# Keys and values of a differential-attention layer: turned by VectorE and DMA in place of TensorE, with the weighted sums as fences in the order of two engines

## The chip, the cores and the metric

The kernel runs on one core of one Trainium2 chip. The metric is the device time of one execution in microseconds (us), the median of several runs; less is better.

## What is computed

One inference step of a trunk of two layers, for a prompt of 512 tokens and 32 sampled tokens, in float32. Layer 0 mixes tokens with RWKV-7, layer 1 with differential attention; both have cross-attention to a memory, a gate and an output projection. The change concerns layer 1 and the norm ahead of it:

```python
def diff_layer(x, mk, mv, k_past, v_past, layer_idx, norm_w, w_out, w_in, lq1, lk1, lq2, lk2, subln):
    h = rmsnorm(x, norm_w)
    q, k, v, qm, gate = jnp.split(h @ w_in, [MIX_W, 2 * MIX_W, 3 * MIX_W, 3 * MIX_W + MEM_W], axis=-1)
    ...
        blocks.append(diff_attention(q[:, s:e], k_all[:, :past + e], v_all[:, :past + e], q_pos, k_pos, lam))
    o = jnp.concatenate(blocks, axis=1)
    o = rmsnorm(o, subln) * (1.0 - lam_init)
    y_mem = mem_attention(qm, mk, mv)
    out = jnp.concatenate([o.reshape(B, T, MIX_W).astype(x.dtype), y_mem], axis=-1) * jax.nn.silu(gate)
    return x + out @ w_out, k, v
```

There are 12 heads of width 128 (two maps of 64 each); `diff_attention` is `softmax(q1 k1) - lam * softmax(q2 k2)`, applied to `v`. Keys and values are outputs too, with the token first and then the head: 512 x 12 x 128 for the prompt and 32 x 12 x 128 for the samples.

## The kernel before

All 544 tokens (512 of the prompt, `TP`, and 32 samples, `TS`) stand as columns; features stand on the 128 partitions. A projection is made in blocks of 128 output features. For float32 accuracy both operands are split into a high and a low part (`hh` and `hl` for the input, `whi` and `wlo` for the weights), and a block is 2 halves of 272 tokens x 8 slices x 3 matmuls = 48 matmuls into `ps_g` (`steps`, line 348). `block` (line 1887) issues these 48 and puts other work between them: `pieces` is a list of (place, step), and a step is issued before the matmul of that place. At the end of a block `used` (line 283) has the weights of a coming block split, ScalarE rounding `whi` and VectorE subtracting to `wlo`, and has SP issue the loads of a later one into `raw`, of which there are five buffers.

`groups` (line 1898) runs layer 1 in three groups of four heads. For a head it issues a block of keys, one of queries and one of values. The head's own attention is a generator (`steps` in `diff_head`, line 2056), which is advanced by the pieces: four steps in its block of values, five in the next head's block of keys and four in the next head's block of queries (gate and memory blocks take their place after the fourth head). The steps of a head, before:

- the keys are rounded, and their parts sent to the other half of the partitions (`kh`, a DMA) and subtracted (`kz`, VectorE);
- in the values' block: `turned(k, 4)`, the scores of the first and second 128 tokens (`scores`: four matmuls, the maximum on VectorE, the exponential on ScalarE, and `combine` on VectorE), then the samples' scores and `probs(0)`, TensorE transposes of the combined probabilities into `aT`;
- in the next block, at places 10, 20, 30, 40 and 45: `turned(v, 5)` and the samples' keys and values; `scores(2)` and `probs(1)`; `weighted(0)`; `scores(3)`; `probs(2)`;
- in the block after that, at 6, 18, 30 and 42: `weighted(1)`, `weighted(2)`, `probs(3)`, `weighted(3)`.

`turned` (line 2017) makes four TensorE transposes of 128 x 128 into `ps_kv`, a ScalarE copy to `kt` or `vt`, and one DMA from there to the output. `ps_kvs` takes two more transposes a head, of the last 128 columns of keys and values, from which ScalarE copies the 32 samples to `vs`. `weighted(t)` (line 2047) sums t + 1 products of `aT` and `vt` in the one buffer of `ps_o`; VectorE copies it to `ot`, and ScalarE sums its squares.

Which order do the instructions take? In layer 0 every instruction is tied to the one before on its engine (`tie`, line 123, while `ordered` is true). In layer 1 `ordered` is false: the framework's scheduler places each engine's instructions, from the order of their issue and what it thinks of their times. Line 106 in the profile stands for all four queues' instructions, since one helper issues them; they are told apart by tile.

Between the layers the input of layer 1 is normalised, slice by slice of 128 features: `h` on VectorE, `hh` rounded by ScalarE, `hl` subtracted by POOL (line 1763). The projections of the memory, with weights of their own to split, are issued between the slices.

Of the kernel before, what the change touches and what calls it, by code (L numbers as in the profile page):

```python
# [97 lines left out]
class Queue:  # L98


    def __init__(self, trunk, engine):
        self.trunk, self.engine, self.last = trunk, engine, None

    def __getattr__(self, name):
        issue = getattr(self.engine, name)
# [3 lines left out]
class Trunk:  # L109
# [13 lines left out]
    def tie(self, queue, ins):  # L123

        if self.ordered:
            if queue.last is not None:
                self.order(ins, queue.last)
            queue.last = ins
        return ins

    def rsqrt(self, y, x, pool, tag):
# [1308 lines left out]
    def layer0(self, mem):  # L1440
# [245 lines left out]
        with ExitStack() as ctx:  # L1686
# [70 lines left out]
            for k in range(KT):  # L1757
                h = p.tile([P, T], F32, tag="hn", name="hn", bufs=HNB)
                for q, c, n in ((0, 0, TP), (1, TP, TS)):
                    self.ve.scalar_tensor_tensor(h[:, c : c + n], self.x1[:, k, c : c + n], self.nw[1][:, k : k + 1],  # L1760
                                                   pr[q][:, :n], ALU.mult, ALU.mult)
                self.ae.copy(self.hh[:, k, :], h[:])
                nc.gpsimd.tensor_tensor(self.hl[:, k, :], h[:], self.hh[:, k, :].bitcast(F32), ALU.subtract)  # L1763
                next(kv, None)
            for _ in kv:
                pass
# [17 lines left out]
    def layer1(self):  # L1784
# [7 lines left out]
        with ExitStack() as ctx:  # L1792
            with ExitStack() as c2:
                self.dfp = p = self.pool("df", 1, ctx=c2)
                m1 = c2.enter_context(ExitStack())
                mp = self.pool("mem1a", 1, ctx=m1, side="right")

                nlam = self.nlam
                self.qs = [p.tile([P, P], F32, name=f"qs{i}") for i in range(2)]
                for t in self.qs:  # L1800
                    nc.gpsimd.memset(t[:], 0.0)
                self.kz = [p.tile([P, 2, T], F32R, name=f"kz{i}") for i in range(2)]
                for t in self.kz:
# [12 lines left out]

                self.groups(w, p, mp, nlam, aside, free)
# [80 lines left out]
    def groups(self, w, p, mp, nlam, aside, free):  # L1898

        late = []  # L1900
        for hg in range(3):
# [5 lines left out]
            def gate(c0, pieces):  # L1907
                self.gates += 1
                sg, _, evac = self.gate_evac(self.gates)
                self.block(w, 3 * MIXW + 512 + c0, evac, pieces)  # L1910
                return sg

            for j, (parts, it) in enumerate(heads):
                h = 4 * hg + j
                before = step(prev, 10, 20, 30, 40, 45) if j else late
                k, q, v = parts()
                self.block(w, MIXW + h * P, k, before)
                if not j and hg == 2:
                    free()
                next(it)  # L1920
                self.block(w, h * P, q, step(prev, 6, 18, 30, 42) if j else ())
                if j:
                    aside()
                if j == 3 and hg < 2:
                    mem = [self.mem_turn(1, 2 * hg + i, mp) for i in range(2)]
                    for _ in range(2):
                        next(mem[0][1])
                self.block(w, 2 * MIXW + h * P, v, step(it, 6, 16, 28, 40))
                prev = it
            end = self.diff_end(gr, nlam)  # L1930
            fin = lambda j, at: (at, lambda: end.send((j, sgs[j])))
            g0 = 4 * hg * P
            sgs.append(gate(g0, step(prev, 10, 20, 30, 40, 45)))
            if hg == 2:
                sgs.append(gate(g0 + P, step(prev, 6, 18, 30, 42)))
                aside()
                sgs.append(gate(g0 + 2 * P, step(end, 2, 10, 18) + [fin(0, 22), fin(1, 36)]))
                sgs.append(gate(g0 + 3 * P, [fin(2, 16)]))
                fin(3, 0)[1]()
                break  # L1940
# [8 lines left out]
                    st["evac"](ps, v)  # L1949
                return evac  # L1950

            self.block(w, 3 * MIXW + st0["c"], query(st0), step(m0, 2) + step(prev, 6, 18, 30, 42))
# [16 lines left out]
    def diff_group(self, hg, p):  # L1969

        a, gr = self.a, {"hg": hg, "on": []}
        gr["ck"] = p.tile([P, 4, P], F32, tag="ck", name="ck")
        gr["cv"] = p.tile([P, 4, P], F32, tag="cv", name="cv")
        gr["ckT"] = p.tile([P, 4, P + TS], F32, tag="ckT", name="ckT")
        gr["vs"] = p.tile([TS, 2, 4, P], F32, tag="vs", name="vs")
        gr["ssb"] = p.tile([P, 2, 160], F32, tag="ssb", name="ssb")
        gr["ss"] = p.tile([P, 3, 16], F32, tag="oss", name="oss")
        return gr
# [6 lines left out]
    def diff_head(self, gr, j, p, nlam):  # L1985
# [29 lines left out]
            return keys, queries, values  # L2015

        def turned(x, n):
            t = p.tile([P, 4, P], F32, tag="kt" if n == 4 else "vt", name="kt" if n == 4 else "vt", bufs=n - 3)
            ps = self.psm.tile([P, 512], F32, tag="m", name="ps_kv")
            for i in range(4):  # L2020
                self.te.transpose(ps[:, i * P : i * P + P], x[:, i * P : i * P + P], self.ident[:])
            self.ae.copy(t[:], ps[:].rearrange("p (j c) -> p j c", j=4))
            self.se.dma_start(o[n][0, 0, :, h, :].rearrange("(i p) d -> p i d", p=P), t[:])
            return t

        def scores(t):
            n, S = (t + 1) * P, []
# [11 lines left out]
        def probs(t):  # L2039
            n = (t + 1) * P  # L2040
            ps = self.psm.tile([P, 512], F32, tag="m", name="ps_aT")
            for i in range(t + 1):
                self.te.transpose(ps[:, i * P : i * P + P], st["pt", t][:, 0, i * P : i * P + P], self.ident[:])
            st["aT", t] = p.tile([P, 512], F32, tag="aT", name="aT", bufs=2)
            self.ae.copy(st["aT", t][:, :n], ps[:, :n])

        def weighted(t):
            aT, ot = st["aT", t], st["ot"]
            po = self.psx.tile([P, 512], F32, tag="x", name="ps_o")
            for i in range(t + 1):  # L2050
                self.te.matmul(po[:, :P], aT[:, i * P : i * P + P], st["vt"][:, i, :], start=i == 0, stop=i == t)
            self.ve.tensor_copy(ot[:, t, :], po[:, :P])
            jk = p.tile([P, P], F32, tag="jk", name="jk", bufs=2)
            self.ae.activation(jk[:], ot[:, t, :], AF.Square, accum_out=gr["ss"][:, 0, 4 * j + t : 4 * j + t + 1])

        def steps():
# [26 lines left out]
            yield  # L2083
            if j == 0:
                self.cached(gr, "v")
            st["vt"] = turned(st["v"], 5)
            ps = self.psm.tile([P, 512], F32, tag="m", name="ps_kvs")
            for i, x in enumerate((k, st["v"])):
                self.te.transpose(ps[:, i * P : i * P + P], x[:, T - P :], self.ident[:])
            self.ae.copy(gr["vs"][:, :, j, :], ps[P - TS :, :256].rearrange("p (j c) -> p j c", j=2))  # L2090
            st["ot"] = p.tile([P, 4, P], F32, tag="ot", name="ot", bufs=4)
            gr["on"].append(st["ot"])
            yield
            scores(2)
            probs(1)
            yield
            weighted(0)
            yield
            scores(3)
            yield  # L2100
            probs(2)
            yield
            weighted(1)
            yield
            weighted(2)
            yield
            probs(3)
            yield
            weighted(3)
# [4 lines left out]
    def diff_end(self, gr, nlam):  # L2114
# [1 line left out]
        hg, p, ssb, vs, ss, o = gr["hg"], self.dfp, gr["ssb"], gr["vs"], gr["ss"], self.o  # L2116
        _, srs = self.softmax([ssb[:, m, :] for m in range(2)], P + TS, p, ssb)
        self.combine(ssb, srs, P + TS, nlam)
        for i, n in ((0, 10), (1, 11)):
            self.se.dma_start(o[n][0, 0, :, 4 * hg : 4 * hg + 4, :], vs[:, i])  # L2120
        self.ve.tensor_scalar(ss[:, 1, :], ss[:, 0, :], 1.0 / P, EPS, ALU.mult, ALU.add)
        self.rsqrt(ss[:, 2, :], ss[:, 1, :], p, "nt16")
        ps = self.psm.tile([P, 512], F32, tag="m", name="ps_saT")
        self.te.transpose(ps[:, :P], ssb[:, 0, :P], self.ident[:])
        self.te.transpose(ps[:TS, P : 2 * P], ssb[:, 0, P:160], self.ident[:])
        aT = p.tile([P, 512], F32, tag="aT", name="aTs", bufs=2)
        self.ae.copy(aT[:, :P], ps[:, :P])
        self.ae.copy(aT[:TS, P : 2 * P], ps[:TS, P : 2 * P])
        yield
# [4 lines left out]
                             tile_position=(0, 32 * j))  # L2134
        for j in range(4):
            rj = slice(32 * j, 32 * j + 32)
            self.te.matmul(po[rj, :P], aT[:TS, P + 32 * j : P + 32 * j + 32], vs[:, 1, j, :], start=False, stop=True,
                             tile_position=(0, 32 * j))
        os_ = p.tile([P, P], F32, tag="os", name="os")
        self.ve.tensor_copy(os_[:], po[:, :P])  # L2140
# [105 lines left out]
```

## Time and profile before

| | us |
|---|---|
| median of 3 runs | 1371.52 (1371.49 to 1371.97) |
| the profiled execution | 1371.42 |
| its span, first to last instruction | 1369.2 |
| POOL `hl<-hn,hh`, 8 times | 12.2 in all, 1.536 each |
| ScalarE `kt<-ps_kv`, 12 times | 0.580 each |
| ScalarE `vt<-ps_kv`, 12 times | 0.588 each |
| the granted clock of TensorE | 0.998 of full speed |

The profile names engines: PE is TensorE's matmuls, PEld its weight loads, DVE VectorE, ACT ScalarE, POOL GpSimd, SP the queue that issues the DMAs. A row of the timeline gives the start, the duration, the engine, the line, the operation with the tiles that it writes and reads, the shape and a count; idle time of the engine before it, and what ended that, stand in brackets. A matmul's duration is longer than the distance to the next one, as matmuls are pipelined: its price is read from starts.

### The profile page before, as it was taken

The page shows a single profiled execution, that of the slowest core. Times are in us where ns is not written, and L with a number is a line of the kernel's source. Part 1 is how long each engine was busy: PE and PEld are TensorE (multiplying, and loading weights), DVE is VectorE, ACT ScalarE, POOL GpSimd, SP SyncE. Part 2 cuts the span into 40 slices and gives each one's busy share as a digit, 9 for nine tenths or more (in the row PEclk, how much of TensorE's full clock was granted, in tenths as well). Part 3 has the DMA queues.
Part 4 walks back from the last instruction along what each step waited for, and adds up shares of the span by engine and source line. Part 5 has one row for each costly group of instructions (what it writes and reads, how often), then busy time and mean ns, then how long its engine had stood idle before and what let it go on. Part 6 is the DMA issues. An engine that isn't in the chain of part 4 may idle for free. (4 is left out here: it accounts for less than half of the span.)

```text
span 1369.2 us, 31861 instructions
## 1 busy us (share of the span) xinstructions
PE 1339.3 (98%) x11845; PEld 1283.9 (94%) x11845; DVE 939.7 (69%) x2353; ACT 822.6 (60%) x2288; POOL 381.9 (28%) x841
## 2 busy tenths in 40 slices
PE   8999999999999999999999999999999999999997
PEld 6988899999999998988999989999999999999997
DVE  5776788888888888667744667775567747667443
ACT  5766777877778777656433466654566537665222
POOL 2138667766686667600000120000000001002000
PEclk9999999999999999999999999999999999999999
DMA  7452322333323332432555563332333323332322
GB/s 224 146 140 70 77 71 57 94 86 74 88 67 84 88 88 64 142 87 76 173 142 147 148 184 88 100 102 82 101 95 94 90 82 94 97 97 79 93 78 73
DMA packets 276964, 139.06 MB, mean 102 GB/s; under 512 B 75769, under 2 KB 265730, under 8 KB 276810
## 3 DMA queue, kind: packets, MB, share of 16 engines
q1 hardware_dynamic: 276746, 137.01, 36.0%
q8 instruction: 94, 1.54, 0.5%
q14 instruction: 60, 0.49, 0.1%
q10 hardware_dynamic: 64, 0.02, 0.0%
HBM read 110.72 MB, written 22.91 MB: 98 GB/s over the span
## 5 line engine op out<-in xcount | busy, mean ns | idle before, releaser
L106 PE MATMUL ps_g<-hh,whi 128*128 128x272 f32 x1808 | 539.7, 299 | 1.0 <-DVE ats L106 0.7
L106 PE MATMUL ps_g<-hh,wlo 128*128 128x272 f32 x1808 | 534.8, 297 | 1.6 <-DVE wlo L106 1.5
L106 PE MATMUL ps_g<-hl,whi 128*128 128x272 f32 x1808 | 532.4, 295 | 0.6 <-DVE hl L106 0.3
L106 PEld LDWEIGHTS ps_g<-hh,whi 128*128 128x128 f32 x1808 | 341.2, 189 | 5.1 <-DVE ats L106 0.9
L106 PEld LDWEIGHTS ps_g<-hh,wlo 128*128 128x128 f32 x1808 | 340.6, 189 | 4.7 <-DVE wlo L106 2.5
L106 PEld LDWEIGHTS ps_g<-hl,whi 128*128 128x128 f32 x1808 | 341.1, 189 | 2.8 <-DVE hl L106 1.3
L106 DVE TENSOR_TENSOR wlo<-raw,whi 128x512 fp32r<-128x512 f32 x314 | 220.1, 712 | 118.3 <-ACT whi L106 114.7
L106 ACT CAST whi<-raw 128x512 fp32r<-128x512 f32 x314 | 188.9, 619 | 115.8 <-PE ps_g L106 62.4
L868 POOL TENSOR_TENSOR tm<-u,m 102x84 f32<-102x84 f32 (+23 forms) x341 | 147.8, 433 | 115.4 <-DMA m<-sc 69.5
L870 POOL TENSOR_TENSOR u<-u,tm 102x84 f32<-102x84 f32 (+23 forms) x341 | 151.6, 445 | 26.6
L106 PE MATMUL ps_g<-hi,wlo 128*128 128x272 f32 x512 | 147.8, 289 | 1.2 <-DVE wlo L106 1.2
L106 PE MATMUL ps_g<-hi,whi 128*128 128x272 f32 x512 | 147.7, 289 | 0.0
L106 PE MATMUL ps_g<-lo,whi 128*128 128x272 f32 x512 | 147.4, 288 | 0.0
L1339 POOL TENSOR_TENSOR lo<-og,hi 128x544 fp32r<-128x544 f32 x8 | 13.2, 1649 | 357.7 <-ACT hi L106 357.2
L106 PEld LDWEIGHTS ps_g<-hi,wlo 128*128 128x128 f32 x512 | 96.4, 188 | 1.7 <-DVE wlo L106 1.6
L106 PEld LDWEIGHTS ps_g<-hi,whi 128*128 128x128 f32 x512 | 96.5, 189 | 0.0
L106 PEld LDWEIGHTS ps_g<-lo,whi 128*128 128x128 f32 x512 | 96.4, 188 | 0.0
L106 ACT ACTIVATE pt<-ps_s,snm 128x128 f32<-128x128 f32 (+3 forms) x96 | 51.0, 532 | 41.7 <-DVE snm L106 41.6
L1763 POOL TENSOR_TENSOR hl<-hn,hh 128x544 fp32r<-128x544 f32 x8 | 12.2, 1536 | 211.4 <-ACT hh L106 211.3
L106 DVE SCALAR_TENSOR_TENSOR SB<-ps_c,dl,sd 64x64 f32<-64x64 f32 x168 | 47.4, 282 | 26.4 <-PE ps_c L106 21.2
L106 ACT COPY sv<-ps_c 64x64 f32<-64x64 f32 x192 | 39.6, 206 | 32.7 <-PE ps_c L106 30.8
L106 ACT ACTIVATE sg<-ps_g 128x272 f32<-128x272 f32 x64 | 25.2, 394 | 41.0 <-PE ps_g L106 38.3
(400 smaller groups left out, 2564.4 us busy)
## 6 DMA issues: line engine op xcount, KB each, us to landing
raw<-in_rw_in_dram SPq DMA_DIRECT2D x114, 256.0 KB
raw<-in_df_in_dram SPq DMA_DIRECT2D x112, 256.0 KB
raw<-in_w_out_dram SPq DMA_DIRECT2D x64, 256.0 KB
oscr<-sg SPq DMA_DIRECT2D x16, 272.0 KB
lo<-oscr SPq DMA_DIRECT2D x16, 272.0 KB
m<-sc SPq DMA_DIRECT2D x33, 128.0 KB
raw<-in_w_mem_v_dram SPq DMA_DIRECT2D x16, 256.0 KB
kh<-kh SPq DMA_DIRECT2D x24, 136.0 KB
```

Source lines behind the costliest of these rows:

```text
L106: return lambda *a, **k: self.trunk.tie(self, issue(*a, **k))
L868: nc.gpsimd.tensor_tensor(tm[:, :n, :wd], u3[:, :n, kx : kx + 1].to_broadcast(sh), m3[:, kx : kx + 1, kx + 1 :].to_broadcast(sh), ALU.mult)
L870: nc.gpsimd.tensor_tensor(u3[:, :n, kx + 1 :], u3[:, :n, kx + 1 :], tm[:, :n, :wd], ALU.add)
L1339: (self.nc.gpsimd if g % 2 and self.o1 else self.ve).tensor_tensor(lo[:], t, hi[:].bitcast(F32), ALU.subtract)
L1763: nc.gpsimd.tensor_tensor(self.hl[:, k, :], h[:], self.hh[:, k, :].bitcast(F32), ALU.subtract)
```

## The change

- **Keys and values.** `turned` makes no TensorE transposes any more. VectorE transposes the 512 prompt columns in blocks of 32 x 32, each in its place, and the 32 sample columns into `new`. Four DMAs, one for each 32 features, write 128-byte pieces and put the blocks in their places: for the keys straight to the output, for the values to a scratch in DRAM (`vscr`, one of two by head). `fetched` reads the values back from there to `vt`, and the values' output is written from `vt`. The samples' values go by four DMAs (`samples`) to `vs`, once a group; their keys go to the output by four DMAs at the end of a group.
- **Order.** The last matmul of each `weighted` is kept as `pin` of TensorE's queue, and its copy as `pin` of VectorE's: every later instruction of that queue is ordered behind it.
- **Places.** In the next block the steps stand at 4, 9, 30 and 44: `turned(v, 5)`; `scores(2)` and `probs(1)`; `fetched` (in the group's last head `samples` as well) and `scores(3)`; `probs(2)`. In the block after at 14, 24, 34 and 46: `weighted(0)` and the values' output; `weighted(1)`; `weighted(2)` and `probs(3)`; `weighted(3)`.
- **Buffers.** Three `aT` for two. The cached keys `ck` and the turned values share one buffer, `vb`.
- **Norm.** `hl` is subtracted by VectorE.

```diff
@@ class Queue, Trunk.tie
-        self.trunk, self.engine, self.last = trunk, engine, None
+        self.trunk, self.engine, self.last, self.pin = trunk, engine, None, None
...
             queue.last = ins
+        elif queue.pin is not None:
+            self.order(ins, queue.pin)
         return ins
@@ layer0, norm
-                nc.gpsimd.tensor_tensor(self.hl[:, k, :], h[:], self.hh[:, k, :].bitcast(F32), ALU.subtract)
+                self.ve.tensor_tensor(self.hl[:, k, :], h[:], self.hh[:, k, :].bitcast(F32), ALU.subtract)
@@ layer1
+                self.vscr = [self.dp.tile([TP, P], F32, name=f"vscr{i}") for i in range(2)]
@@ groups (the gate and memory blocks that take the same steps likewise)
-                before = step(prev, 10, 20, 30, 40, 45) if j else late
+                before = step(prev, 4, 9, 30, 44) if j else late
...
-                self.block(w, h * P, q, step(prev, 6, 18, 30, 42) if j else ())
+                self.block(w, h * P, q, step(prev, 14, 24, 34, 46) if j else ())
@@ diff_group
-        gr["ck"] = p.tile([P, 4, P], F32, tag="ck", name="ck")
+        gr["ck"] = p.tile([P, 4, P], F32, tag="vb", name="ck")
...
-        gr["vs"] = p.tile([TS, 2, 4, P], F32, tag="vs", name="vs")
+        gr["vs"] = p.tile([TS, 4, P], F32, tag="vs", name="vs")
+        gr["new"] = p.tile([P, 2, 4, TS], F32, tag="new", name="new")
@@ diff_head
         def turned(x, n):
-            t = p.tile([P, 4, P], F32, tag="kt" if n == 4 else "vt", name="kt" if n == 4 else "vt", bufs=n - 3)
-            ps = self.psm.tile([P, 512], F32, tag="m", name="ps_kv")
-            for i in range(4):
-                self.te.transpose(ps[:, i * P : i * P + P], x[:, i * P : i * P + P], self.ident[:])
-            self.ae.copy(t[:], ps[:].rearrange("p (j c) -> p j c", j=4))
-            self.se.dma_start(o[n][0, 0, :, h, :].rearrange("(i p) d -> p i d", p=P), t[:])
+            t = p.tile([P, 4, P], F32, tag="kt" if n == 4 else "vb", name="kt" if n == 4 else "vb")
+            t = t[:].rearrange("p j c -> p (j c)")
+            self.ve.transpose(t, x[:, :TP])
+            self.ve.transpose(gr["new"][:, n - 4, j, :], x[:, TP:])
+            to = o[4][0, 0, :, h, :] if n == 4 else self.vscr[h % 2][:]
+            to = to.rearrange("(b i) (a c) -> a i b c", i=TS, c=TS)
+            for a in range(4):
+                r = slice(TS * a, TS * a + TS)
+                self.se.dma_start(to[a], t[r, :].rearrange("i (b c) -> i b c", c=TS))
+
+        def fetched():
+            t = p.tile([P, 4, P], F32, tag="vt", name="vt", bufs=2)
+            self.se.dma_start(t[:], self.vscr[h % 2][:].rearrange("(i p) d -> p i d", p=P))
             return t
+
+        def samples():
+            for a in range(4):
+                r = slice(TS * a, TS * a + TS)
+                self.se.dma_start(gr["vs"][:, :, r], gr["new"][r, 1])
...
         def weighted(t):
...
-                self.te.matmul(po[:, :P], aT[:, i * P : i * P + P], st["vt"][:, i, :], start=i == 0, stop=i == t)
-            self.ve.tensor_copy(ot[:, t, :], po[:, :P])
+                mm = self.te.matmul(po[:, :P], aT[:, i * P : i * P + P], st["vt"][:, i, :], start=i == 0, stop=i == t)
+            cp = self.ve.tensor_copy(ot[:, t, :], po[:, :P])
+            self.te.pin, self.ve.pin = mm, cp
...
-            st["vt"] = turned(st["v"], 5)
-            ps = self.psm.tile([P, 512], F32, tag="m", name="ps_kvs")
-            for i, x in enumerate((k, st["v"])):
-                self.te.transpose(ps[:, i * P : i * P + P], x[:, T - P :], self.ident[:])
-            self.ae.copy(gr["vs"][:, :, j, :], ps[P - TS :, :256].rearrange("p (j c) -> p j c", j=2))
+            turned(st["v"], 5)
...
             scores(2)
             probs(1)
             yield
-            weighted(0)
-            yield
+            st["vt"] = fetched()
+            if j == 3:
+                samples()
             scores(3)
             yield
             probs(2)
             yield
+            weighted(0)
+            self.se.dma_start(o[5][0, 0, :, h, :].rearrange("(i p) d -> p i d", p=P), st["vt"][:])
+            yield
             weighted(1)
             yield
             weighted(2)
-            yield
             probs(3)
@@ diff_end
-        for i, n in ((0, 10), (1, 11)):
-            self.se.dma_start(o[n][0, 0, :, 4 * hg : 4 * hg + 4, :], vs[:, i])
+        self.se.dma_start(o[11][0, 0, :, 4 * hg : 4 * hg + 4, :], vs[:])
+        for a in range(4):
+            r = slice(TS * a, TS * a + TS)
+            self.se.dma_start(o[10][0, 0, :, 4 * hg : 4 * hg + 4, r], gr["new"][r, 0])
```

More of the change, by code (lines that the diff above doesn't have):

```diff
@@ L1932, in groups @@
             g0 = 4 * hg * P
-            sgs.append(gate(g0, step(prev, 10, 20, 30, 40, 45)))
+            sgs.append(gate(g0, step(prev, 4, 9, 30, 44)))
             if hg == 2:
-                sgs.append(gate(g0 + P, step(prev, 6, 18, 30, 42)))
+                sgs.append(gate(g0 + P, step(prev, 14, 24, 34, 46)))
                 aside()
@@ L1950, in query @@
                 return evac
-            self.block(w, 3 * MIXW + st0["c"], query(st0), step(m0, 2) + step(prev, 6, 18, 30, 42))
+            self.block(w, 3 * MIXW + st0["c"], query(st0), step(m0, 2) + step(prev, 14, 24, 34, 46))
             sgs.append(gate(g0 + P, step(end, 8, 20, 44)))
@@ L2043, in probs @@
                 self.te.transpose(ps[:, i * P : i * P + P], st["pt", t][:, 0, i * P : i * P + P], self.ident[:])
-            st["aT", t] = p.tile([P, 512], F32, tag="aT", name="aT", bufs=2)
+            st["aT", t] = p.tile([P, 512], F32, tag="aT", name="aT", bufs=3)
             self.ae.copy(st["aT", t][:, :n], ps[:, :n])
@@ L2125, in diff_end @@
         self.te.transpose(ps[:TS, P : 2 * P], ssb[:, 0, P:160], self.ident[:])
-        aT = p.tile([P, 512], F32, tag="aT", name="aTs", bufs=2)
+        aT = p.tile([P, 512], F32, tag="aT", name="aTs", bufs=3)
         self.ae.copy(aT[:, :P], ps[:, :P])
@@ L2136, in diff_end @@
             rj = slice(32 * j, 32 * j + 32)
-            self.te.matmul(po[rj, :P], aT[:TS, P + 32 * j : P + 32 * j + 32], vs[:, 1, j, :], start=False, stop=True,
+            self.te.matmul(po[rj, :P], aT[:TS, P + 32 * j : P + 32 * j + 32], vs[:, j, :], start=False, stop=True,
                              tile_position=(0, 32 * j))
```

## The prediction

> **What bounds the kernel now.** I read the page first, then the busy times by stage, then TensorE's waits, then single stretches of the timeline. The profiled execution took 1371.42 us around a span of 1369.2 us, so 2.2 us lie outside the span; the median of the three runs is 1371.52 us. The sum below is made against 1371.42.
>
> ```profile
> span 1369.2 us, 31861 instructions
> PE 1339.3 (98%) x11845; PEld 1283.9 (94%) x11845; DVE 939.7 (69%) x2353; ACT 822.6 (60%) x2288; POOL 381.9 (28%) x841
> ```
>
> By stage (window, its length, then busy time and instruction count of PE, PEld, DVE, ACT and POOL, clock, DMA share, GB/s):
>
> ```profile
> 760.00:800.00 40.00, 37.18 (x292) 34.87 (x291) 32.45 (x60) 22.22 (x52) 13.30 (x12) 1.00 0.53 155
> 799.00:1256.00 457.00, 456.56 (x3605) 446.39 (x3604) 300.15 (x842) 266.77 (x796) 7.29 (x10) 1.00 0.34 97
> ```
>
> The second row is layer 1's block stage: TensorE is busy for all but 0.44 us of 457, at full clock, while VectorE and ScalarE have a third to spare and the DMA engines two thirds. Busy time of a pipelined engine can hide small gaps, so the price of an instruction is read from starts. The first row is the passage between the layers, where the normalised input is made; there TensorE does wait:
>
> ```profile
> PE ps_g L106 <- DVE wlo L106: 1.5, 2, 1.0
> ```
>
> So in layer 1 an instruction taken from TensorE shortens the run by what it holds TensorE, unless something else arrives later. That "unless" is the whole question.
>
> **Transposes off TensorE.** One evacuation group of values in the timeline of PE (start, duration):
>
> ```profile
> 984.25 0.60 PE L106 MATMUL ps_kv<-ident,v 128*128 128x128 f32 x4
> 984.69 0.27 PE L106 MATMUL ps_kvs<-ident,k 128*128 128x128 f32 x1
> 984.80 0.27 PE L106 MATMUL ps_kvs<-ident,v 128*128 128x128 f32 x1
> 984.83 0.37 PE L106 MATMUL ps_g<-hl,whi 128*128 128x272 f32 x1
> 985.03 0.29 PE L106 MATMUL ps_g<-hh,wlo 128*128 128x272 f32 x1
> ...
> 986.03 0.28 PE L106 MATMUL ps_g<-hl,whi 128*128 128x272 f32 x1
> ```
>
> From 985.03 to 986.03 eight block matmuls start: 0.125 us each (a block is 48 of them). From 984.25 to 985.03 lie six transposes and one block matmul: 0.78 - 0.125 = 0.655, so 0.109 us a transpose. Their number:
>
> ```profile
> L106 PE MATMUL ps_kv<-ident,k x48: 270/272/275, 810.6 to 1217.4; 128*128 128x128 f32 x48
> ...
> L106 PE MATMUL ps_kv<-ident,v x48: 270/272/273, 819.3 to 1225.7; 128*128 128x128 f32 x48
> ```
>
> That is 4 + 4 in each of 12 heads, and the code adds the two `ps_kvs` ones a head: 120 x 0.109 = 13.1 us, all on the path. The three ScalarE copies a head that emptied them go too; ScalarE is not the bound, so I count nothing for them.
>
> The Trainium skill (VectorE: DVE Perf Modes, section Rules for kernel authors) says the contrary of this edit: for a 128x128 transpose use TensorE where a PSUM destination will do. Followed here the transposes stay and the time stays 1371.4; the rows above decide, since TensorE is the one engine with nothing to spare.
>
> **What VectorE takes on.** The same operation stands in layer 0:
>
> ```profile
> L106 DVE STREAM_TRANSPOSE x<-xr x8: 735/738/739, 688.4 to 761.5; 128x544 f32<-128x544 f32 x8
> ```
>
> So 0.74 us at most for 512 columns; the 32-column one costs between nothing and 0.74, and I take 0.1, in proportion to its columns. Two of each a head are 1.7 us more, in a head whose block matmuls alone take 3 x 48 x 0.125 = 18 us, on an engine with a third free. Keys have no reader but the output, so their turn and four stores cost nothing unless something queues behind them: on SP they take the place of one store after the block's second weight load, and the next weight load is a block away.
>
> **The trip of the values.** They go to DRAM in 128-byte pieces and come back before the first weighted sum, on which every later matmul now queues. Head 5's stretch of the block after its values (PE, ACT, DVE, SP):
>
> ```profile
> 1009.62 0.60 PE L106 MATMUL ps_kv<-ident,v 128*128 128x128 f32 x4
> ...
> 1011.53 0.34 PE L106 MATMUL ps_s<-kh,qp 128*128 128x384 f32 x1
> 1011.71 0.34 PE L106 MATMUL ps_s<-kz,qp 128*128 128x384 f32 x1
> ...
> 1015.18 0.40 PE L106 MATMUL ps_s<-kh,qp 128*128 128x512 f32 x1
> 1015.41 0.40 PE L106 MATMUL ps_s<-kz,qp 128*128 128x512 f32 x1
> ```
> ```profile
> 1013.82 0.61 ACT L106 ACTIVATE pt<-ps_s,snm 128x384 f32<-128x384 f32 x1
> ```
> ```profile
> 1009.08 1.50 DVE L106 TENSOR_TENSOR wlo<-raw,whi 128x512 fp32r<-128x512 f32 x2 [0.18 <-ACT whi L106]
> 1012.13 0.11 DVE L106 MEMSET ps_s<- 64x64 f32 x1 [1.56 <-PE ps_s L106]
> ...
> 1012.98 0.56 DVE L106 TENSOR_REDUCE snm<-ps_s 128x1 f32<-128x384 f32 x1
> 1014.13 0.29 DVE L106 COPY ot<-ps_o 128x128 f32<-128x128 f32 x1 [0.59 <-PE ps_o L106]
> ```
> ```profile
> 1009.80 1.17 SPq L106 DMA_DIRECT2D raw<-in_df_in_dram  x2
> 1011.06 0.46 SPq L106 DMA_DIRECT2D out_dram<-vt  x1
> ```
>
> The values' transposes stand ten matmuls into the block, which therefore began at 1009.62 - 1.25 = 1008.37. *When are they wanted?* The first weighted sum moves to 14 matmuls into the next block: 62 x 0.125 = 7.75 us of block matmuls, plus the scores put between (4 x 0.18 and 4 x 0.23 us) and five transposes of probabilities (0.55): 1008.37 + 7.75 + 2.19 = 1018.31. *When do they come?* VectorE is free of its two weight subtractions at 1009.08 + 1.50 = 1010.58, turns the values by 1011.32, and SP has been free since 1010.97. Then, from layer 0 (SP issues, and POOL, which waited for their landing):
>
> ```profile
> 713.38 2.09 SPq L106 DMA_DIRECT2D xr<-in_x_prompt_dram  x4
> ```
> ```profile
> 323.67 2.40 SPq L106 DMA_DIRECT2D sc<-u  x6
> ...
> 327.22 2.16 SPq L106 DMA_DIRECT2D m<-sc  x6
> ```
> ```profile
> 327.77 0.48 POOL L862 CAST u<-ui 102x352 f32<-102x352 bf16 x1 [4.86 <-DMA sc<-u]
> 332.44 0.24 POOL L868 TENSOR_TENSOR tm<-u,m 102x31 f32<-102x31 f32 x1 [4.19 <-DMA m<-sc]
> ```
>
> Four issues of the shape wanted take 2.09 us: 1013.41. The stores `sc<-u`, which the code makes in rows of 32 floats, had landed 327.77 - 326.07 = 1.70 us after the last issue: 1015.11. SP stands still for those 1.70 us; behind it wait the next weight loads, which the pattern above (first load 1.43 us into a block) makes due only at about 1018. The fetch is issued in 0.46 us: 1015.57. A read back from DRAM, `m<-sc`, was in use 332.44 - 329.38 = 3.06 us after its last issue; that is the upper end, the store's 1.70 the lower. I take 2.7, near the read: 1018.27. Wanted 1018.31, there 1018.27: a dead heat. With the transpose slipped between the two subtractions and 1.70 for the read it is there at 1016.5; with 3.06, and the cached values' load (0.46) issued ahead as in each group's first head, at 1019.1, a wait of 0.8 us. I take 0.2 us a head on average: 12 x 0.2 = 2.4 us.
>
> A second place is tight for the same reason. The scores moved to matmul 9 begin at 1009.5, but VectorE is busy until about 1011.4, so their maxima start some 1.3 us later behind their matmuls than the 0.60 us of 1011.53 to 1012.13. The next scores follow after 21 x 0.125 + 0.94 = 3.57 us and need the two banks back. Before, the second bank was given back at 1014.43 and wanted at 1015.65, so 1.3 us of delay leaves a wait of about 0.1. It isn't added: it moves the weighted sum's due time by as much. The fences' own price: a weighted sum's bank must be copied before the next one, ten matmuls = 1.25 us later. Before, the first sum stood thirty matmuls into the block, at 1008.37 + 3.75 + 0.66 + 0.72 + 0.22 = 1013.72, and its copy ran from 1014.13 for 0.29: 0.7 us in all, so VectorE may come 0.5 us late without cost. On VectorE the fence holds everything issued later behind that copy, the next weight subtractions above all; those are for the block after next, so nobody waits for them at once. Nothing added; up to 0.2 us a sum if VectorE is busier than that.
>
> The rest is small. In a group's last head four copies of the samples' values stand on SP behind the fetch, and the end of a group makes five stores in place of two: at 0.52 us an issue 2.1 and 1.6 us of SP, ahead of loads that are due one block or more later. The third buffer for probabilities and the tile shared by cached keys and turned values add no wait that I can see, since the cached keys are read long before the group's first values are turned. Nothing for these.
>
> **The norm's low parts.** Eight subtractions of 544 columns go from POOL to VectorE. VectorE's weight subtractions between the layers, and in layer 1 (count | busy, mean ns):
>
> ```profile
> L106 DVE TENSOR_TENSOR wlo<-raw,whi 128x512 fp32r<-128x512 f32 x12 | 12.8, 1093 | 1.2 <-ACT whi L106 1.2
> ```
> ```profile
> L106 DVE TENSOR_TENSOR wlo<-raw,whi 128x512 fp32r<-128x512 f32 x83 | 58.2, 704 | 34.7 <-ACT whi L106 32.8
> ```
>
> While POOL works, the same instruction takes 0.39 us longer; 12 x 0.39 = 4.7 us come back, against 8 x 0.70 x 544/512 = 6.0 us added. About even, on an engine nearly full there. One thing may cost beside: VectorE now stands while ScalarE rounds each tile, unless other work is put between. Bounds: the 40.00 - 37.18 = 2.8 us that TensorE idles in that window gained, or 6.0 lost. I take nothing.
>
> The sum: 1371.4 - 13.1 + 2.4 + 0 = 1360.7 us.
>
> **The rivals.**
>
> *The trip is late by more than it saves.* If VectorE takes the moved scores' maxima (1012.13 to 1013.54, 1.41 us) ahead of the values' transpose, the values come at 1019.68 and TensorE waits 1.37 us in each head, because the fence lets no block matmul pass: 12 x 1.37 = 16.4, 1374.7 us, slower. The point where it turns is 13.1 / 12 = 1.09 us a head. For it: the dead heat, and one engine doing all the new work just there. Against: the values are ready before the scores are.
>
> *Short pieces are slow.* If a store in 128-byte pieces took twice the 1.70 us, the wait would be 1.9 us a head, 22.8 in all: 1381 us. Against it: the 1.70 is itself of such pieces, though of fewer. The Trainium skill (DMA: Bandwidth & Descriptors, Specifications) asks for at least 512 B and says that below it a read-modify-write is made; by that rule this is the case to expect, and the 1.70 us does not bear it out.
>
> *VectorE bounds the passage between the layers.* If nothing is given back there, the norm costs 6.0 us; with 0.5 us of wait a head, 1371.4 - 13.1 + 6.0 + 6.0 = 1370.3, no change.
>
> That the transposes stay is ruled out by the code.
>
> **How the numbers follow.** Forecast 0.75, late trip 0.12, short pieces 0.04, norm 0.09. The forecast's own range is 1355.5 us (1371.4 - 13.1 - 2.8: no wait, and the passage's idle time gained) to 1368.0 (0.8 us a head). To hold 8 in 10 it reaches to the norm's case: 1355.5 to 1371.0, leaving 0.16 above. A measurement of this kernel tells 0.2%, 2.7 us, from no change. Faster 0.75, same 0.09, slower 0.16.
>
> **What would show it.** Right: no `ps_kv` or `ps_kvs` on PE; a head's period shorter by about 0.9 us; in the row for the block stage still nearly no idle time of PE; small waits of `ps_o` on `vt` in the first head of each group. Wrong: PE waiting for the DMA into `vt` in every head by over 1 us (late trip), `ps_s` waiting for VectorE, or PE waiting for `wlo` or `hl` between 777 and 800 by more than now (norm). A wait of `ps_o` on `ot` would say that the fences cost.

## The result, and the profile after

The changed kernel takes 1396.38 us (median of 4 runs, 1395.82 to 1398.12) against 1371.72 before on the same chip: ratio 1.0176, 95% interval 1.0164 to 1.0188. It is slower by 24.7 us, where 10.7 less was forecast. In the profiled execution (1396.17 us) the transposes are gone as foreseen, 120 matmuls fewer, but TensorE's idle time has grown from 29.9 to 58.2 us:

```profile
span 1394.4 us, 31684 instructions
PE 1336.2 (96%) x11725; PEld 1275.1 (91%) x11725; DVE 948.1 (68%) x2409; ACT 807.7 (58%) x2252; POOL 366.3 (26%) x833
```

By stage (window, length, busy time and count of PE, PEld, DVE, ACT, POOL, clock, DMA share, GB/s):

```profile
760.00:800.00 40.00, 38.91 (x316) 37.61 (x315) 30.88 (x68) 23.57 (x54) 2.53 (x6) 1.00 0.64 184
799.00:1280.00 481.00, 450.69 (x3452) 433.81 (x3451) 308.23 (x888) 251.02 (x757) 4.40 (x5) 0.99 0.42 104
```

The passage between the layers lost 1.7 us of its 2.8 us of idle time. The loss is all in layer 1's block stage, where before TensorE was idle for 0.44 us and is now for 30. From the first block matmul of layer 1 to the last it is 460.35 us before and 487.97 after: +27.6, so beside the 13.1 us saved there are 40.7 us of new cost. What TensorE waited for in that stage (us in total, times, longest):

```profile
PE ps_o L106 <- DMA vt<-vscr: 15.2, 6, 6.2
PE ps_o L106 <- DVE ot L106: 9.7, 7, 1.5
PE ps_s L106 <- ACT pt L106: 4.4, 9, 0.7
```

Three waits, then, none of which was there before. The period of a head (from one `ps_sc` to the next) tells where: 25.37 us before; 26.75 in the first two groups of heads; 26.92, 33.77 and 33.93 in the third.

**The first two groups: copies.** Head 5's first two weighted sums on PE, and VectorE at that time:

```profile
1020.63 0.38 PE L106 MATMUL ps_o<-vt,aT 128*128 128x128 f32 x2
1023.75 0.71 PE L106 MATMUL ps_o<-vt,aT 128*128 128x128 f32 x4 [1.50 <-DVE ot L106]
```
```profile
1020.70 1.29 DVE L106 TENSOR_TENSOR wlo<-raw,whi 128x512 fp32r<-128x512 f32 x2
1021.91 1.47 DVE L106 TENSOR_TENSOR kz<-k,kh 64x544 fp32r<-64x544 f32 x2
1023.41 0.29 DVE L106 COPY ot<-ps_o 128x128 f32<-128x128 f32 x1
```

The values are there: the first sum starts without a wait. Its copy, however, stands behind two weight subtractions and the two `kz` of the next head and starts 2.78 us after the sum. The second sum needs the bank, and nothing that comes later may pass it.

**The same groups: scores.** At the end of the head VectorE stands before its fence:

```profile
1029.27 0.29 DVE L106 COPY ot<-ps_o 128x128 f32<-128x128 f32 x1 [2.54 <-PE ps_o L106]
1029.59 0.71 DVE L106 STREAM_TRANSPOSE kt<-k 128x512 f32<-128x512 f32 x1
...
1032.79 0.19 DVE L106 MEMSET ps_s<- 64x64 f32 x2
```
```profile
1033.84 0.38 PE L106 MATMUL ps_s<-kh,qp 128*128 128x256 f32 x1 [0.42 <-ACT pt L106]
```

It idles 2.54 us for the last weighted sum; the keys' turn, the subtractions and the queries behind it then come all at once, ahead of the mask of the first scores (1032.79, 1.47 us after the scores' first matmul at 1031.32). The second scores wait for these banks. By starts the copy costs 1.66 us in this head and the scores 0.57. The four score matmuls behind such a wait take 0.69 us, where 0.50 were taken before, since two of them start 0.22 us after the one ahead instead of 0.117. That is 2.4 together, nearly all of the 2.47 us by which 26.75 exceeds 25.37 - 1.09.

**The third group: the fetch.** SP, what it waited for between 1185 and 1192, and PE:

```profile
1183.51 2.05 SPq L106 DMA_DIRECT2D vscr<-vb  x4
1191.14 0.39 SPq L106 DMA_DIRECT2D raw<-in_df_in_dram  x1
1191.64 0.47 SPq L106 DMA_DIRECT2D kh<-kh  x1
1192.29 0.45 SPq L106 DMA_DIRECT2D vt<-vscr  x1
```
```profile
SPq L106 <- DVE wlo L106: 5.5, 1, 5.5
```
```profile
1196.87 0.79 PE L106 MATMUL ps_o<-vt,aT 128*128 128x128 f32 x2 [6.19 <-DMA vt<-vscr]
```

In this group's second and third head the plan (the order that the scheduler chose) has put a weight load and a transfer of `kh` ahead of the fetch. The load waits 5.5 us for the buffer that VectorE's subtraction frees, and TensorE stands 6.19 us. The price goes on after that (windows as above):

```profile
1190.00:1197.00 7.00, 0.81 (x7) 0.59 (x5) 3.70 (x6) 2.30 (x5) 0.00 (x0) 0.77 0.59 144
1197.00:1200.50 3.50, 3.50 (x17) 3.50 (x17) 0.41 (x2) 0.79 (x3) 0.00 (x0) 0.50 0.38 95
1200.50:1204.00 3.50, 3.50 (x31) 3.50 (x30) 1.35 (x4) 1.65 (x6) 0.00 (x0) 0.98 0.00 0
```

After the idle stretch the granted clock is half, and 17 matmuls pass in 3.5 us where 31 pass in the next 3.5.

Two such waits are 12.4 of the 15.2 us. The other four are one of 0.42 us and three, of 0.65 to 1.08, in the last heads of the groups. In the first group's last head SP shows

```profile
899.43 2.68 SPq L106 DMA_DIRECT2D vs<-new  x4
902.28 0.46 SPq L106 DMA_DIRECT2D vt<-vscr  x1
```

The four copies of the samples' values are ahead of the fetch, though the code issues them behind it; the first sum starts at 905.97, after 0.66 us of waiting. With the copies behind the fetch (e3 below) this wait is 0.16 us, and in the last heads of the other two groups there is none.

### The profile page after: what moved, and what is told of

Same layout as the page of the kernel before. It is cut to its first block, busy times and chain, and to the rows that moved or that the text cites. A ratio compares the mean times of both kernels' runs of the same rounds, so it can differ in the third digit from the quotient of the medians.

```text
span 1394.4 us, 31684 instructions
## 1 busy us (share of the span) xinstructions
PE 1336.2 (96%) x11725; PEld 1275.1 (91%) x11725; DVE 948.1 (68%) x2409; ACT 807.7 (58%) x2252; POOL 366.3 (26%) x833
## 5 line engine op out<-in xcount | busy, mean ns | idle before, releaser
L106 DVE TENSOR_TENSOR wlo<-raw,whi 128x512 fp32r<-128x512 f32 x314 | 213.6, 695 | 100.1 <-ACT whi L106 97.9
L872 POOL TENSOR_TENSOR u<-u,tm 102x84 f32<-102x84 f32 (+23 forms) x341 | 147.3, 432 | 26.6
L106 PE MATMUL ps_o<-vt,aT 128*128 128x128 f32 x240 | 37.3, 288 | 24.9 <-DMA vt<-vscr 15.2
L106 PEld LDWEIGHTS ps_o<-vt,aT 128*128 128x128 f32 x240 | 32.2, 197 | 27.8 <-DMA vt<-vscr 16.5
```

Source lines behind the costliest of these rows:

```text
L106: return lambda *a, **k: self.trunk.tie(self, issue(*a, **k))
L872: nc.gpsimd.tensor_tensor(u3[:, :n, kx + 1 :], u3[:, :n, kx + 1 :], tm[:, :n, :wd], ALU.add)
```

## The experiments

The theory before the first of them: the fences cost, by the waits that they put in the way of everything later (on TensorE, the block matmuls behind a late sum; on VectorE, what waits behind a copy). The rivals: the transposes were not worth 0.109 us each, or the norm's low parts cost. All but the last two were timed beside the kernel before at 1371.8 to 1372.4; the last two at 1372.5.

**The norm's low parts alone** (e1), on the kernel before:

```
-  nc.gpsimd.tensor_tensor(self.hl[:, k, :], h[:], self.hh[:, k, :].bitcast(F32), ALU.subtract)
+  self.ve.tensor_tensor(self.hl[:, k, :], h[:], self.hh[:, k, :].bitcast(F32), ALU.subtract)
```

> The kernel before with one edit: the norm's low parts on VectorE. The trace of after begins layer 1's first block at 793.72 us, that of before at 796.07, with the memory's first matmul at 765.69 and 765.55. Theory A, the norm's move gives these 2.4 us and nothing is paid later: about 1369.3 us. Theory B, the gain came from elsewhere, or VectorE pays it back: 1371.5 or more.

Measured 1369.9 us, ratio 0.9981 (0.9971 to 0.9991): a gain of about 2 us, theory A, and not a cost. Between 777 and 797 us VectorE shows in the changed kernel:

```profile
L106 DVE TENSOR_TENSOR wlo<-raw,whi 128x512 fp32r<-128x512 f32 x12 | 7.8, 687 | 0.0
L106 DVE TENSOR_TENSOR hl<-hn,hh 128x544 fp32r<-128x544 f32 x7 | 5.1, 722 | 0.4 <-ACT hh L106 0.4
```

The subtractions are back from 1093 to 687 ns, and the new ones stood 0.4 us for ScalarE in all (e1's own trace: 689 ns and 0.3 us).

**Without both fences** (e2):

```
-            self.te.pin, self.ve.pin = mm, cp
```

> After without the two fences; all else stays. Theory A, the loss of after (about 40 us of new waits in layer 1) comes from what the scheduler puts ahead of two instructions, the fetch on SP and the copies on VectorE, and from one bank for the weighted sums: without fences the sums move back behind more block matmuls, so the 16 us of waits for the fetched values and some 3.5 us at half clock go, the 11 us of waits for the copy may stay: 1370 to 1380 us. Theory B, the fences alone make the loss: about 1356 us. Theory C, the trip of the values is too long whatever the order: 1390 us or more.

Measured 1362.96 us, ratio 0.9934 (0.9919 to 0.995), between theories A and B. The same work, without that line, is 33 us faster than with it and 9 faster than before. Of the three waits 0.3 us for `vt` remain; a head is 24.80 us, 0.57 less than before where 1.09 was expected. Where the missing 0.52 went can be seen in head 2 (PE, then VectorE's copies):

```profile
855.21 0.38 PE L106 MATMUL ps_o<-vt,aT 128*128 128x128 f32 x2
856.05 0.71 PE L106 MATMUL ps_o<-vt,aT 128*128 128x128 f32 x4
```
```profile
855.71 0.29 DVE L106 COPY ot<-ps_o 128x128 f32<-128x128 f32 x1
856.80 0.29 DVE L106 COPY ot<-ps_o 128x128 f32<-128x128 f32 x1 [0.80 <-PE ps_o L106]
```

Left to itself the plan runs the four sums close together, four to six block matmuls apart, and the second starts as its forerunner's copy ends (856.00 and 856.05). By starts the sums take 6.55 us in three heads where they took 5.70, 0.28 a head. The block matmuls take as much again over what they take with two banks for the sums (e9 below: 18.80 us a head against 19.08).

**The fetch ahead of the loads** (e3): what comes later on SP stays behind the fetch.

```
-            self.se.dma_start(t[:], self.vscr[h % 2][:]...)
+            self.se.pin = self.se.dma_start(t[:], self.vscr[h % 2][:]...)
```

> After, with the fetch of the values as a fence in SP's order too: no later load can stand ahead of it. Theory A (in the last group the next weight load and the keys' copies stand ahead of the fetch on SP, which costs two waits of 6.2 us, one of 1.1, and the half clock behind them): about 16 us less, 1380 us, and no wait for the fetched values over 1 us. Theory C (the trip itself is too long): 1394 us or more, waits of 1 us and more for the fetched values in most heads.

Measured 1385.14 us, ratio 1.0095 (1.0079 to 1.0111): 11 us less than the change, not 16. The waits for `vt` are gone but for 0.7 us, and those for copies have grown instead:

```profile
PE ps_o L106 <- DVE ot L106: 14.2, 11, 2.0
```

So the late fetch is shown for the third group, and it had covered part of the copies' lateness there.

**Four columns of one bank** (e4): a head's four sums in four quarters of the bank, so that no sum writes over another.

```
+            if not t:
+                st["po"] = self.psx.tile([P, 512], F32, tag="x", name="ps_o")
+            po = st["po"][:, t * P : t * P + P]
```

> After, with the four weighted sums of a head in four quarters of one bank, so that a sum needn't wait for the copy of the one before. Theory A (the copy stands behind two weight subtractions and two key subtractions on VectorE, and the next sum waits for its bank, 7 heads by about 1.6 us): 11 us less, 1385.5 us, no wait of ps_o for ot within a head. Theory D (VectorE as a whole is behind, and TensorE waits for it elsewhere instead): 1394 us or more, with more waits of ps_s or ps_g for VectorE.

Measured 1395.83 us, ratio 1.0179 (1.0162 to 1.0196), and the wait for the copies stands at 9.8 us where it was 9.7. A miss: it was meant to take the wait away and did not, so it does not tell the theories apart. The Trainium skill (PSUM — Partial Sum Buffer, section PSUM bank collisions raise a hardware error) says that the scheduler makes any two instructions of different engines on one bank and the same partitions wait for each other, whatever the columns; the 9.8 us agree with it, though a wait that the framework keeps for a whole tile would look the same. The two banks below are the test that this was to be.

**One fence at a time** (e5 and e6):

```
-            self.te.pin, self.ve.pin = mm, cp
+            self.te.pin = mm          # e5; in e6: self.ve.pin = cp
```

> The change with TensorE's fence alone: matmuls still stay behind a weighted sum's last matmul, VectorE's instructions no longer stay behind its copy. Theory A (the loss sits in VectorE's order: the copy of a weighted sum stands behind weight subtractions and the next one needs its bank; TensorE's order by itself costs little): the waits of the weighted sums on their copies, 9.7 us in the changed kernel, fall under 2, and since VectorE's weight subtractions and so the loads move too, the time is 1365 to 1380. Theory B (TensorE's order is what costs: matmuls that could fill a wait may not pass): 1388 to 1396, with the wait for the fetched values still near 15 us.

> The change with VectorE's fence alone: nothing holds block matmuls behind a weighted sum. Theory A (VectorE's order costs): the copies still stand behind subtractions, the weighted sums' waits on their copies stay above 5 us in sum, and the time is 1380 or more. Theory B (TensorE's order costs): about the time without both fences, 1361 to 1367.

TensorE's alone: 1409.31 us, ratio 1.0274 (1.0255 to 1.0292), worse than both together, and worse than either theory allowed. VectorE's alone: 1373.2, ratio 1.0005 (0.9996 to 1.0015), between the theories and 10 us over none. TensorE's fence is by far the dearer, by one mechanism:

```profile
PE ps_o L106 <- DMA vt<-vscr: 32.2, 11, 3.4
```

SP shows why in head 2:

```profile
856.20 0.32 SPq L106 DMA_DIRECT2D out_dram<-kt  x1
856.70 0.38 SPq L106 DMA_DIRECT2D vt<-vscr  x1
```

With VectorE free again the plan is another one, and on SP a store of the *next* head's turned keys, which VectorE makes only then, is queued ahead of this head's fetch. Without a fence on TensorE the sums are put behind more block matmuls (e2 has 0.3 us of this wait); with it TensorE stands up to 3.4 us in 11 heads. With VectorE's fence alone no sum waits for a copy and one waits for its values, 1.5 us in the third group; the scores' banks are waited for (3.7 us in 8 times).

**Two banks for the sums** (e7), both fences kept; the orders on TensorE and VectorE are those of the change, instruction by instruction.

```
-            po = self.psx.tile([P, 512], F32, tag="x", name="ps_o")
+            po = self.psm.tile([P, 512], F32, tag="m", name="ps_o")
```

> The change as it is, fences and every engine's order kept, but a weighted sum is written to the pool of two PSUM banks that the turned keys and values have left, in place of the pool of one. Theory A (the single bank makes a weighted sum wait for the copy of the one before): the 9.7 us of waits on copies go and nothing takes their place, 1386. Theory B (the time is VectorE's, which is late whichever bank is used, so the wait moves to the probabilities' or scores' banks): over 1393.

Measured 1391.59 us, ratio 1.0139 (1.0124 to 1.0154): 4.8 us less than the change, half of what the theory of the single bank said. The second sum no longer waits, but the third user of the two banks, the transposes `ps_aT`, does:

```profile
PE ps_aT L106 <- DVE ot L106: 3.4, 6, 0.6
```

So it is the copy that is late; a bank more lets it be later before that costs.

**The keys alone** (e8), on the kernel before: `turned(k, 4)` by VectorE and four stores, the samples' keys from the turned tile, the values on TensorE as before. In e12 the same, with the sums in the pool of two banks and every third tile of scores in the bank that these left:

```
+                if (2 * t + m) % 3 == 2:
+                    ps = self.psx.tile([P, 512], F32, tag="x", name="ps_s")
```

> The kernel before with the keys alone turned by VectorE and DMA (the samples' keys too); values, places and orders of the weighted sums as before, no fence. It takes 12 x 5 = 60 transposes from TensorE. Theory A (0.109 us a transpose, all on the path): 1371.7 - 6.5 = 1365.2, 1363.5 to 1367. Theory B (half of the price was hidden, as the kernel without fences, 8.8 us faster for 13.1 forecast, would suggest): 1368 to 1370.

Measured 1370.26 us, ratio 0.9985 (0.9976 to 0.9995): of 6.5 us some 2 arrive, as theory B had it. But by starts the four transposes and the `ps_kvs` did give back 0.47 us a head. The scores took 0.28 of it: in head 2 PE and VectorE show

```profile
863.97 0.22 PE L106 MATMUL ps_s<-kh,qp 128*128 128x128 f32 x1
...
866.07 0.38 PE L106 MATMUL ps_s<-kh,qp 128*128 128x256 f32 x1
866.29 0.28 PE L106 MATMUL ps_s<-kz,qp 128*128 128x256 f32 x1
```
```profile
863.91 0.69 DVE L106 TENSOR_TENSOR wlo<-raw,whi 128x512 fp32r<-128x512 f32 x1
864.63 0.44 DVE L106 SCALAR_TENSOR_TENSOR qp<-ps_g,qp 64x272 fp32r<-64x272 f32 x1
865.09 0.11 DVE L106 MEMSET ps_s<- 64x64 f32 x1
```

VectorE comes to the first scores 1.12 us after their matmul; the second ones find their banks taken and start 0.22 us apart in place of 0.117.

> The kernel before with the keys alone turned by VectorE and DMA, weighted sums in the pool of two banks and scores round three. Theory A (the keys' turn was worth 6.5 us, and 0.4 us a head of it went into waits for the scores' two banks, because VectorE came to the first scores one weight subtraction later): 1370.3 - 12 x 0.4 = 1365.5, 1364 to 1367. Theory B (those waits are not what eats it): 1369 to 1371.

Measured 1366.12 us, ratio 0.9958 (0.9942 to 0.9974), with 24.86 us a head: theory A. With a third bank for scores the keys' turn is worth 6.0 of the 6.5 us that 0.109 us a transpose makes. The second bank for the sums, which e12 adds too, is not what gave it: by starts the sums take 1.90 us a head in e8 and in e12, and no sum waits for a copy in either; the scores take 2.81 and 2.56.

**No fence, two banks** (e9) **and three** (e10):

> The change without both fences, and the weighted sums written to the pool of two PSUM banks. Theory A (without fences the four sums of a head run close together, each waits for the copy of the one before, and that took 0.3 us a head of the gain): 1363.0 - 12 x 0.3 = 1359.4, 1358 to 1361. Theory B (the missing gain is elsewhere; a transpose is worth less than 0.109 us): 1362 to 1364.

> As the one before, and every third tile of scores is written to the bank that the weighted sums have left, so that scores go round three banks instead of two. Theory A (the scores' two banks are what every step that makes VectorE later runs into): without fences hardly any wait for the scores' banks is left, so this is worth under 1 us: 1358 to 1361. Theory B (more of the head is held up by these banks than the waits show): 2 us or more under the run without the third bank.

Measured 1360.59 us, ratio 0.9922 (0.9904 to 0.994), and 1360.57, ratio 0.9918 (0.99 to 0.9936). The single bank under the bunched sums cost some 2 us (0.19 a head), the third bank of the scores changes nothing here. A head is 24.61 us: by starts the turns of keys and values, off TensorE, are 0.93 us and fewer joints in the block 0.18, together 1.11 beside the 1.09 of the prediction; the sums, still near each other, take 0.37 back. This is the fastest version found, 11.5 us under the kernel before and 36 under the change. PE's waits in the stage are three, of 0.2 to 0.4 us.

**Both fences, with something against each of the three waits** (e11: the fetch ahead, two banks, three banks), and this with one fence (e13: TensorE's, e14: VectorE's):

> The change with both fences, the fetch of the values held ahead of later loads on SP, weighted sums in two banks, scores in three. Theory A (the three waits are the fences' whole cost: the late fetch, the copy's bank, the scores' banks): all three go and the time is 1360 to 1367, about that without fences. Theory B (a fence costs whatever the buffers are, since what is held up on VectorE and TensorE is late for the next step): 1375 to 1385.

> As the run with both fences and all three waits mended, without VectorE's fence: TensorE's order alone, the fetch held ahead on SP, two banks for weighted sums, three for scores. Theory A (what is left there, 11 us over the run without fences, comes of VectorE's order, which puts subtractions and copies ahead of what the banks wait for): 1360 to 1364. Theory B (it comes of TensorE's order): 1368 to 1372.

> The same without TensorE's fence: VectorE's order alone, the fetch held ahead, two banks and three. Theory A (VectorE's order is what is left): 1368 to 1372. Theory B (TensorE's order is): 1360 to 1364.

With both: 1371.62 us, ratio 0.9996 (0.9987 to 1.0006), between the theories: 25 of the 36 us between the change and the fastest version are gone, 11 stay. The waits are shorter or moved, not gone; in e11 PE shows 9.9 us of them:

```profile
PE ps_aT L106 <- DVE ot L106: 3.9, 7, 0.6
PE ps_o L106 <- DMA vt<-vscr: 3.0, 3, 1.4
PE ps_s L106 <- ACT pt L106: 3.0, 9, 0.7
```

I put the 11 us on VectorE's order, wrongly: with that fence alone it is 1363.0 (0.9928, 0.9912 to 0.9945), which these intervals don't tell from no fence at all (e10), and with TensorE's alone 1372.51 (1.0003, 0.9993 to 1.0012). In e13 PE waits for copies, and VectorE's rows are the known ones:

```profile
PE ps_aT L106 <- DVE ot L106: 5.6, 10, 0.6
PE ps_o L106 <- DVE ot L106: 5.3, 10, 0.7
```
```profile
1017.30 1.29 DVE L106 TENSOR_TENSOR wlo<-raw,whi 128x512 fp32r<-128x512 f32 x2
...
1020.10 0.25 DVE L106 COPY ot<-ps_o 128x128 f32<-128x128 f32 x1
```

VectorE has no fence here and takes the four subtractions (two `wlo`, then two `kz` at 1018.50) ahead of the copy all the same. The 10.9 us of these two waits are the 12 us between 1372.5 and 1360.6 to within one. So what is left is TensorE's order: the sums are held to places at which VectorE has other work, and no block matmul may go ahead of them. The fences were not run with the sums at other places, so how much of the price belongs to these places is open.

## Why the prediction was wrong, point by point

- *120 transposes at 0.109 us, 13.1 us.* Right in size (e12; the starts in e9), and on the path. In the changed kernel it is there too, under 40.7 us of new cost.
- *VectorE's turns cost nothing.* The long ones' durations were right (0.70 to 0.71 us, 0.74 said at most); the 32-column ones took 0.17 to 0.21 us, where 0.1 was put (in proportion to the columns it would have been 0.05). That nothing comes of them was wrong wherever the scores' two banks were left: 0.4 us a head with the keys alone (e8 against e12).
- *The trip of the values, a dead heat.* Right in the first two groups, where three of eight heads waited, 1.7 us in all. In head 5 the four stores took 2.20 us (2.09 said), the fetch was issued 2.20 us later (1.70 said), and its data landed 2.62 us after the issue (2.7 said); the first sum did not wait. Twice the 1.70 us, the case of the short pieces, would have been 3.40. The Trainium skill (DMA: Bandwidth & Descriptors, Specifications) names a read-modify-write for pieces under 512 B; these 2.20 us show no doubled time.
- *"behind it wait the next weight loads, which the pattern above ... makes due only at about 1018"* Failed. In the third group the plan puts a load ahead of the fetch, and SP waits for that load's buffer: 5.5 us, and 11 us of the run's time by e3. The prediction counted what the fetch delays, not what may be put before it. "In a group's last head four copies of the samples' values stand on SP behind the fetch" fell likewise: they stand ahead of it, for 0.65 to 1.08 us of wait.
- *Scores' banks, a wait of about 0.1, not added.* Mis-sized and misplaced: 0.4 us of wait, some 0.8 by starts, and at the scores of the second 128 tokens, whose forerunners VectorE reaches late because the fence bunched its work.
- *"The fences' own price ... Nothing added; up to 0.2 us a sum if VectorE is busier than that."* This is the step that failed worst. The line costs 33 us (e2). Before, VectorE came to the copy 0.4 us after the first sum; the sum was then moved to a place where two `wlo` and two `kz` stand, and the 0.5 us of slack read from the old place did not hold at the new one. The prediction asked who waits for the subtractions behind a copy ("nobody"), and not which subtractions stand ahead of it, nor that the first scores' maxima are among what is held up behind the last copy. The same pile stood in the kernel before, two `wlo` (1019.67 and 1020.93) and two `kz` ahead of the copy of head 5's third sum (PE's third and fourth sum, then VectorE):

```profile
1020.14 0.83 PE L106 MATMUL ps_o<-vt,aT 128*128 128x128 f32 x6
...
1024.25 1.05 PE L106 MATMUL ps_o<-vt,aT 128*128 128x128 f32 x8
```
```profile
1021.53 1.46 DVE L106 TENSOR_TENSOR kz<-k,kh 64x544 fp32r<-64x544 f32 x2
1023.03 0.29 DVE L106 COPY ot<-ps_o 128x128 f32<-128x128 f32 x1
```

There the copy came 2.89 us after its sum and nobody waited, because the plan had put the next sum 4.11 us behind. With TensorE's fence the next sum comes after ten block matmuls, whatever VectorE is doing.
- *The norm's low parts, about even.* Between -2.8 and +6.0 us it came out at -2 (e1). The Trainium skill (SBUF — State Buffer, section SBUF: two separate sides) names a port pair that VectorE and GpSimd lock against each other; the 1093 ns beside POOL's work and 687 without it agree.
- *The rivals.* Late trip: its sign and its reason "the fence lets no block matmul pass" held, its place (VectorE takes the scores' maxima first) did not. Short pieces and the norm's case: not borne out. The sign the prediction said would tell of the fences, a wait of `ps_o` on `ot`, is what came.

That the forecast and the version without fences lie at 1360.7 and 1360.6 is no merit: the forecast had 2.4 us of waits for the fetch, that version has some 4 us of crowded sums, and 2 gained at the norm.

## What to carry to other kernels

A line that only orders instructions is not free: price it as every wait that it turns from "something else goes first" into "the engine stands", and read what stands *ahead* of the fenced instruction at its new place, on its engine and on the queue that feeds it. When a step is moved, the slack must be read again at the new place. When work leaves the bound engine, look at the buffers that the engine taking it must give back in time; the freed PSUM banks were worth 4 us in e12 against e8.

## What the runs showed of the hardware

An idle stretch of 6.2 us on TensorE was followed by about 3.6 us at half the granted clock (0.50 in the window from 1197, 0.98 from 1200.5), which adds about 1.8 us to each such wait. The Trainium skill (TensorE: Matmul & The Clock Gate, Part 1: The HAM clock gate) tells of an idle window and a busy window of about 3.4 us each and a clock of 4/8 between them; the rows agree. In e5, with 11 waits of up to 3.4 us, seven stretches of 3.41 or 6.83 us are at half clock, so not every wait of that length does it. Of the score matmuls behind a wait for a bank, two (the changed kernel) or three (e8) of four start 0.22 us after the one ahead in place of 0.117, so that a wait costs more by starts than its row says; whether the weight load is what is then no longer hidden was not tried.
